# A hybrid decoder layer on one core: first-stage stores on GpSimd's queue, layer norm of two thirds on VectorE in column slices

## The chip, the cores and the metric

One Trainium2 chip, one core of it. The time is the device time of one execution in microseconds (us); a kernel's time is the median over its runs. Engines are named as the profile names them: PE (TensorE, matmuls; PEld its weight loads), DVE (VectorE), ACT (ScalarE), POOL (GpSimd) and SP (SyncE, which issues most DMAs).

## What is computed

One inference step of a decoder layer for 1024 prompt rows and 64 sample rows (together T = 1088), model width 2048, all in fp32:

```
h = x @ w_in + b_in              # q, k, v of two attention mixers, gates z and g: 78 tiles of 128 columns
q, k = rope(q), rope(k)          # first quarter of each head
o_a = sliding-window attention (window 128, sinks); o_b = 3 dilated groups, combined by their log-denominators
y_a, y_b = o_a * silu(z_a), o_b * silu(z_b)
m = sigmoid(g_a) * (y_a @ w_br_a) + sigmoid(g_b) * (y_b @ w_br_b)
y = LayerNorm(alpha * x + m @ w_out) * ln_g + ln_b
```

Besides y, the k and v of the step and the caches shifted by 8 rows are outputs, so part of the work is copying the old caches from HBM to HBM.

## The kernel before, in words

Every fp32 matrix product is made of three fp32r products: each operand is split into a rounded part (hi) and a rest (lo). For the weights this is done on the fly: SP loads 512 KB of weights into `wraw` (L78), ACT casts a piece of 128x512 to `whi` (L89), DVE subtracts it to get `wlo` (L90), and PE works on that piece (a "unit") with twelve matmuls. `Weights.ahead` (L100) asks for pieces some units ahead of PE, as far as 4 (first stage) or 6 (last stage) buffers of `whi` and `wlo` and 2 or 3 of `wraw` allow.

The order is written out by hand: one engine's instructions run in the order in which the program emits them. `tick` (L136) counts steps of PE's work, and `after(n, f)` (L132) emits f's instructions n ticks later. One tick is one unit against one chunk of columns in the first two stages (twelve matmuls), one whole unit in the last.

1. **First stage** (0 to about 861 us): `in_proj` (L164) over 34 tiles of q, k and v, twelve ticks each, columns in three chunks (384, 384, 320). `evac_qkv` (L266) takes each chunk out of PSUM, applies rope, and splits q and k into `hi` and `lo`, which have one buffer each, so the next tile writes where this one was. `store` (L310, L347) and `store_kv` (L328) then write to HBM: five DMAs for each of 20 q tiles, eleven for each of 7 k tiles, seven for each of 7 v tiles. `tick_q` (L371) adds a copy of a piece of old cache (up to 510 KB) every fourth tick, 96 in all. All these 322 DMAs are issued by SP, in one order with the weight loads.
2. **Second stage** (to about 2114 us): `in_proj` over the 44 gate tiles, with attention, decoding and merging emitted beside it, a step per tick. GpSimd does the attention's reductions over partitions (L446, L460) and issues the decode's loads. The attention's first loads are L396 (k), L409 (q) and L403 (v).
3. **Last stage**: three thirds of the columns, `CHUNKS`. For each third a *branch part* of 16 feature tiles, three units each (L1015 to L1017, 48 ticks; after each tile DVE does L1023, L1024, L1025 and, behind ACT's cast L1027, L1031), then an *output part* with 64 units (L1058 to L1060). After it `evac_out` (L1066) forms h and its statistics. The norm of the last third is done at the end of the program; the norm of the first two thirds is put into the next third's branch part, by `after` at the loop's end (L1115 to L1119): `norm_start` (L972) on DVE, then `norm_beside` (L984) on GpSimd, four operations of 128x2048 for each of three row tiles, and one store of 1 MB per tile.

Of the kernel before, what the change touches and what calls it, by code (L numbers as in the profile page):

```python
# [19 lines left out]
P = 128  # L20
DM = 2048
KT = DM // P
NT = 1024
NB = 8
NQ = 8
# [3 lines left out]
HD = 64  # L29
# [76 lines left out]
def layer_kernel(ctx: ExitStack, tc: tile.TileContext, A, O, S):  # L106
    nc = tc.nc
# [24 lines left out]
    def after(n, f):  # L132

        later.append((now[0] + n, f))
# [75 lines left out]
    with tc.tile_pool(name="qp", bufs=2, side="right") as qp:  # L210
# [55 lines left out]
        def evac_qkv(ft, c, a, b, pt):  # L266
            kind, idx, dil = FT[ft]
            n, e = b - a, min(b, NT)
            m = e - a
            bcol = bias[:, ft:ft + 1]  # L270
            if kind == "v":
                if c == 0:
                    held["f"] = qp.tile([P, T], F32, tag="kv", name="kvf", bufs=3)
                f = held["f"]
                nc.scalar.activation(cm(f, dil, a, e), nat(pt, dil, m), AF.Identity, bias=bcol)
                if e < b:
                    nc.scalar.activation(f[:, NT:], pt[:, m:n], AF.Identity, bias=bcol)
                    after(2, lambda: store_kv(1, idx, dil, f))
                    for h in range(2):
                        after(2 + h, lambda h=h: split_v(idx, f, h))  # L280
                return
            raw = qp.tile([P, 384], F32, tag="raw", name="raw")
            sw = qp.tile([P, 384], F32, tag="sw", name="sw")
            nc.scalar.activation(raw[:, :n], pt[:, :n], AF.Identity, bias=bcol)
            nc.vector.stream_shuffle(sw[:, :n], raw[:, :n], SWAP)
            nc.vector.tensor_mul(raw[:, :n], raw[:, :n], cost[:, a:b])
            nc.vector.tensor_mul(sw[:, :n], sw[:, :n], sint[:, a:b])
            if c == 0:
                held["hi"] = qp.tile([P, NT], F32R, tag="hi", name="qhi", bufs=1)
                held["lo"] = qp.tile([P, NT], F32R, tag="lo", name="qlo", bufs=1)  # L290
                if kind == "k":
                    held["f"] = qp.tile([P, T], F32, tag="kv", name="kvf", bufs=3)
            hi, lo, f = held["hi"], held["lo"], held.get("f")
            if kind == "q":
                nc.vector.tensor_add(raw[:, :n], raw[:, :n], sw[:, :n])
                src = nat(raw, dil, m)
            else:
                src = cm(f, dil, a, e)
                nc.vector.tensor_add(src, nat(raw, dil, m), nat(sw, dil, m))
                if e < b:  # L300
                    nc.vector.tensor_add(f[:, NT:], raw[:, m:n], sw[:, m:n])

            def split():
                nc.scalar.copy(cm(hi, dil, a, e), src)
                nc.vector.tensor_tensor(out=cm(lo, dil, a, e), in0=src, in1=cm(hi, dil, a, e).bitcast(F32),
                                        op=ALU.subtract)
                if e < b:
                    after(3, store)

            def store():  # L310
                if kind == "q":
                    nc.sync.dma_start(out=S["sq"][idx], in_=raw[:, m:n])
                    for t, x in enumerate((hi, lo)):
                        for h in range(2):
                            nc.sync.dma_start(out=S["qs"][idx, h, HD * t:HD * (t + 1)],
                                              in_=x[HD * h:HD * (h + 1)].bitcast(F32))
                else:
                    for t, x in enumerate((hi, lo)):
                        for j in range(4):
                            r = HD * (j // 2)  # L320
                            nc.sync.dma_start(out=S["ks"][2 * idx + j // 2, t, HD * (j % 2):HD * (j % 2 + 1)],  # L321
                                              in_=x[r:r + HD].bitcast(F32))
                    store_kv(0, idx, dil, f)
                    nc.sync.dma_start(out=S["sk"][idx], in_=f[:, NT:])

            after(1, split)

        def store_kv(kv, idx, dil, f):  # L328
            g, i = (0, 0) if idx == 0 else (1 + (idx - 1) // 2, (idx - 1) % 2)
            w = min(NT, 128 if g == 0 else WINS[g - 1])  # L330
            j = NT // dil
            nc.sync.dma_start(
                out=O[f"kv{g}"][kv, i].rearrange("p (c j) -> p c j", c=dil),
                in_=f[:, :NT].rearrange("p (c j) -> p c j", c=dil)[:, :, j - w // dil:])
            nc.sync.dma_start(out=O[f"kvs{g}"][kv, i], in_=f[:, NT:])

        def split_v(idx, f, half):
            pt = psa()
# [3 lines left out]
            v = pt.rearrange("p (j h d) -> p j h d", j=4, h=2)  # L342
# [3 lines left out]

            def store():  # L347
                for h in range(2):
                    nc.sync.dma_start(
                        out=S["vs"][2 * idx + h, :, 4 * half:4 * half + 4],  # L350
                        in_=vs[:, :, h].rearrange("p j s d -> p j (s d)").bitcast(F32))

# [4 lines left out]
            nc.tensor.transpose(pt[:NS, :P], f[:, NT:], ident)  # L357
            sv = qp.tile([NS, P], F32, tag="sv", name="sv")
            nc.scalar.copy(sv, pt[:NS, :P])
            nc.sync.dma_start(out=S["sv"][idx], in_=sv)  # L360

        copies = []
        for g in range(4):
# [7 lines left out]
        def tick_q():  # L371
            tick()
            if copies and now[0] > 30 and now[0] % 4 == 0:
                g, b, r, e = copies.pop(0)
                nc.sync.dma_start(out=O[f"c{g}"][b, r:e], in_=A[f"c{g}"][b, NQ + r:NQ + e])

        in_proj([ORDER[:2]] + [[ft] for ft in ORDER[2:34]], 0, evac_qkv, tick_q)
        while later or copies:
# [602 lines left out]
        nc.gpsimd.tensor_mul(h, h, lng[:h.shape[0], a:b])  # L981
        nc.gpsimd.tensor_add(h, h, lnb[:h.shape[0], a:b])

    def norm_beside(h, v):  # L984
        nc.gpsimd.tensor_sub(h, h, v[:, 0:1].to_broadcast([P, DM]))  # L985
        nc.gpsimd.tensor_mul(h, h, v[:, 2:3].to_broadcast([P, DM]))
        nc.gpsimd.tensor_mul(h, h, lng)
        nc.gpsimd.tensor_add(h, h, lnb)

    def norm_vector(h, v, a, b):  # L990
        h = h[:, a:b]
        nc.vector.scalar_tensor_tensor(out=h, in0=h, scalar=v[:, 0:1], in1=lng[:h.shape[0], a:b],
                                       op0=ALU.subtract, op1=ALU.mult)
        nc.vector.scalar_tensor_tensor(out=h, in0=h, scalar=v[:, 2:3], in1=lnb[:h.shape[0], a:b],
                                       op0=ALU.mult, op1=ALU.add)

    gi = 78 * 4
    for part, (a, b) in enumerate(CHUNKS):
# [113 lines left out]
        if not last:  # L1112
            after(2, lambda: nc.scalar.activation(m4[:, :, 2], m4[:, :, 1], AF.Sqrt, bias=epst))
            nxt = load_g(0, *CHUNKS[part + 1])
            for i, (t, c) in enumerate(tiles):  # L1115
                h, v = hs[i], mv[:, 4 * i:4 * i + 4]
                after(3, lambda v=v: norm_start(v))
                after(4 + i, lambda h=h, v=v: norm_beside(h, v))
                after(5 + i, lambda t=t, h=h: nc.gpsimd.dma_start(out=O["y"][t:t + P], in_=h))  # L1119
    while later:  # L1120
        tick()

# [127 lines left out]
```

## Time and profile before

| | |
|---|---|
| median of 3 runs | 2870.86 us (2870.16 to 2871.94) |
| the profiled execution | 2865.24 us, its span 2863.5 us |
| mean granted TensorE clock | 0.983 |
| busy share of the span | PE 96%, PEld 92%, DVE 53%, ACT 32%, POOL 27% |
| moved by DMA | 467.60 MB, 163 GB/s over the span |

The profile shows one execution. Its own time is 5.6 us under the median of the runs; spans and waits below are of this execution. The span is the time from its first to its last instruction. PE's busy time counts matmuls in flight, at whatever clock was granted, so a stretch can be long by idle time or by a low clock; the view by stretches shows both.

### The profile page before, as it was taken

The page shows a single profiled execution, that of the slowest core. Times are in us where ns is not written, and L with a number is a line of the kernel's source. Part 1 is how long each engine was busy: PE and PEld are TensorE (multiplying, and loading weights), DVE is VectorE, ACT ScalarE, POOL GpSimd, SP SyncE. Part 2 cuts the span into 40 slices and gives each one's busy share as a digit, 9 for nine tenths or more (in the row PEclk, how much of TensorE's full clock was granted, in tenths as well). Part 3 has the DMA queues.
Part 4 walks back from the last instruction along what each step waited for, and adds up shares of the span by engine and source line. Part 5 has one row for each costly group of instructions (what it writes and reads, how often), then busy time and mean ns, then how long its engine had stood idle before and what let it go on. Part 6 is the DMA issues. An engine that isn't in the chain of part 4 may idle for free.

```text
span 2863.5 us, 42950 instructions
## 1 busy us (share of the span) xinstructions
PE 2760.6 (96%) x16423; PEld 2641.7 (92%) x16423; DVE 1530.0 (53%) x2600; ACT 925.8 (32%) x1857; POOL 770.9 (27%) x589
## 2 busy tenths in 40 slices
PE   8999999999989999999999999999999996997898
PEld 8999999989989999999999998889899886986886
DVE  5444433423426778777665422116556458557856
ACT  4222222222223544444443321223144323432442
POOL 0000000000005666677677613432100025004201
PEclk9999999999999999999999999999999997998899
DMA  6345564465463333455445445559866535643662
GB/s 217 101 126 164 165 187 150 156 190 167 142 198 110 116 111 114 136 153 150 142 144 149 123 119 189 182 168 284 276 202 233 188 120 168 241 131 105 205 220 96
DMA packets 224965, 467.60 MB, mean 163 GB/s; under 512 B 33896, under 2 KB 151208, under 8 KB 221240
## 3 DMA queue, kind: packets, MB, share of 16 engines
q1 hardware_dynamic: 206264, 405.09, 45.0%
q0 software_dynamic: 16400, 52.43, 6.1%
q10 hardware_dynamic: 2096, 7.34, 0.7%
q8 instruction: 129, 2.11, 0.3%
q14 instruction: 76, 0.62, 0.1%
HBM read 365.17 MB, written 144.21 MB: 178 GB/s over the span
## 4 chain that ended last, share of the span: by engine, by line
PE 84%; DVE 6%; DMA 5%; SPq 2%; issue 1%; ACT 1%; POOL 0%; ACTq 0%; DVEq 0%; POOLq 0%
PE psd L170 19%; PE psd L172 18%; PE psd L171 18%; PE psd L1060 3%; PE psd L1059 3%; PE psd L1058 3%; PE psa L425 2%; PE psd L1017 2%; PE psd L1016 2%; PE psd L1015 2%; DMA wraw<-w_in 2%; DVE wlo L90 2%; SPq L321 1%; PE psa L487 1%; PE psa L486 1%
## 5 line engine op out<-in xcount | busy, mean ns | idle before, releaser
L170 PE MATMUL psd<-xhi,whi 128*128 128x384 f32 (+1 forms) x3712 | 1226.2, 330 | 26.4 <-ACT whi L89 23.8
L172 PE MATMUL psd<-xhi,wlo 128*128 128x384 f32 (+1 forms) x3712 | 1219.5, 329 | 2.1 <-DVE wlo L90 1.7
L171 PE MATMUL psd<-xlo,whi 128*128 128x384 f32 (+1 forms) x3712 | 1217.8, 328 | 0.3 <-DVE xlo L226 0.3
L90 DVE TENSOR_TENSOR wlo<-wraw,whi 128x512 fp32r<-128x512 f32 x648 | 482.2, 766 | 653.6 <-ACT whi L89 641.7
L170 PEld LDWEIGHTS psd<-xhi,whi 128*128 128x128 f32 x3712 | 699.9, 189 | 48.9 <-ACT whi L89 26.3
L172 PEld LDWEIGHTS psd<-xhi,wlo 128*128 128x128 f32 x3712 | 699.3, 188 | 5.7 <-DVE wlo L90 5.7
L171 PEld LDWEIGHTS psd<-xlo,whi 128*128 128x128 f32 x3712 | 699.7, 189 | 0.8 <-DVE xlo L226 0.8
L89 ACT CAST whi<-wraw 128x512 fp32r<-128x512 f32 x648 | 385.7, 618 | 592.2 <-DMA wraw<-w_in 348.8
L446 POOL PARTITION_ALL_REDUCE md<-s x160 | 214.6, 1341 | 1038.9 <-DMA vst<-s_vs 865.0
L460 POOL PARTITION_ALL_REDUCE md<-s x160 | 310.0, 1938 | 67.4 <-ACT s L457 44.2
L477 DVE TENSOR_TENSOR pl<-s,ph 128x512 fp32r<-128x512 f32 (+1 forms) x160 | 127.9, 800 | 100.4 <-ACT ph L476 98.4
L1017 PE MATMUL psd<-y,wlo 128*128 128x384 f32 (+1 forms) x384 | 129.1, 336 | 29.7 <-DVE wlo L90 29.7
L985 POOL TENSOR_TENSOR h<-h,mv 128x2048 f32<-128x2048 f32 x6 | 21.6, 3608 | 484.1 <-ACT whi L89 276.3
L1015 PE MATMUL psd<-y,whi 128*128 128x384 f32 (+1 forms) x384 | 129.1, 336 | 21.6 <-ACT whi L89 21.6
L1060 PE MATMUL psd<-wlo,m 128*128 128x512 f32 x384 | 149.8, 390 | 0.0
L1059 PE MATMUL psd<-whi,m 128*128 128x512 f32 x384 | 149.7, 390 | 0.0
L1058 PE MATMUL psd<-whi,m 128*128 128x512 f32 x384 | 149.6, 390 | 0.0
L457 ACT ACTIVATE s<-s 128x256 f32<-128x256 f32 (+1 forms) x160 | 75.9, 475 | 195.9 <-DVE s L456 193.8
L951 ACT ACTIVATE z<-psd,bias 128x384 f32<-128x384 f32 x132 | 73.8, 562 | 195.1 <-PE psd L172 129.4
L1016 PE MATMUL psd<-y,whi 128*128 128x384 f32 (+1 forms) x384 | 128.3, 334 | 0.0
L491 DVE TENSOR_TENSOR num<-psa,pvl 64x256 f32<-64x256 f32 x160 | 66.1, 413 | 77.3 <-ACT pvl L490 76.6
L1017 PEld LDWEIGHTS psd<-y,wlo 128*128 128x128 f32 x384 | 74.4, 194 | 32.1 <-DVE wlo L90 32.1
(202 smaller groups left out, 3183.4 us busy)
## 6 DMA issues: line engine op xcount, KB each, us to landing
wraw<-w_in SPq DMA_DIRECT2D x152, 512.0 KB
wraw<-w_out SPq DMA_DIRECT2D x96, 512.0 KB
wraw<-w_br SPq DMA_DIRECT2D x72, 512.0 KB
o_c<-c SPq DMA_DIRECT2D x64, 510.0 KB
qst<-s_qs SPq DMA_DIRECT2D x80, 256.0 KB
s_zg<-z SPq DMA_DIRECT2D x64, 192.0 KB
kv<-ktb POOLq DMA_DIRECT2D x48, 256.0 KB, 3.4
kv<-vb POOLq DMA_DIRECT2D x48, 256.0 KB, 3.1
```

The costliest lines, as they stand in the source:

```text
L89: self.nc.scalar.copy(hi, raw)
L90: self.nc.vector.tensor_tensor(out=lo, in0=raw, in1=hi.bitcast(F32), op=ALU.subtract)
L170: nc.tensor.matmul(o, lhsT=h, rhs=xhi[k][:, a:b], start=(k == 0), stop=False)
L171: nc.tensor.matmul(o, lhsT=h, rhs=xlo[k][:, a:b], start=False, stop=False)
L172: nc.tensor.matmul(o, lhsT=l, rhs=xhi[k][:, a:b], start=False, stop=(k == KT - 1))
L446: nc.gpsimd.partition_all_reduce(u["md"][:, 0], top, P, RED.max)
L460: nc.gpsimd.partition_all_reduce(u["md"][:, 1], s[:, 1 if n == 1 else 2], P, RED.add)
L1015: nc.tensor.matmul(o, lhsT=h, rhs=yt[k][:, 0, :n], start=st, stop=False)
L1017: nc.tensor.matmul(o, lhsT=l, rhs=yt[k][:, 0, :n], start=False, stop=en)
L1058: nc.tensor.matmul(pt, lhsT=h, rhs=whi, start=st, stop=False)
L1059: nc.tensor.matmul(pt, lhsT=l, rhs=whi, start=False, stop=False)
L1060: nc.tensor.matmul(pt, lhsT=h, rhs=wlo, start=False, stop=en)
```

## The change

Two independent edits. In the first stage every store and every cache copy is issued by GpSimd in place of SP (same transfers, same place in the program). In the last stage the norm of the first two thirds is done by DVE with two `scalar_tensor_tensor` operations per slice of 512 columns (subtract the mean and multiply by ln_g; multiply by the inverse deviation and add ln_b), one operation per tick, with a store of 256 KB per slice from GpSimd; `norm_vector`, which the last third uses, is split into the two functions.

```
         def store():
             if kind == "q":
-                nc.sync.dma_start(out=S["sq"][idx], in_=raw[:, m:n])
+                nc.gpsimd.dma_start(out=S["sq"][idx], in_=raw[:, m:n])
...
-                            nc.sync.dma_start(out=S["qs"][idx, h, HD * t:HD * (t + 1)],
+                            nc.gpsimd.dma_start(out=S["qs"][idx, h, HD * t:HD * (t + 1)],
...
-                            nc.sync.dma_start(out=S["ks"][2 * idx + j // 2, t, HD * (j % 2):HD * (j % 2 + 1)],
+                            nc.gpsimd.dma_start(out=S["ks"][2 * idx + j // 2, t, HD * (j % 2):HD * (j % 2 + 1)],
...
         def tick_q():
...
-                nc.sync.dma_start(out=O[f"c{g}"][b, r:e], in_=A[f"c{g}"][b, NQ + r:NQ + e])
+                nc.gpsimd.dma_start(out=O[f"c{g}"][b, r:e], in_=A[f"c{g}"][b, NQ + r:NQ + e])
...
-    def norm_beside(h, v):
-        nc.gpsimd.tensor_sub(h, h, v[:, 0:1].to_broadcast([P, DM]))
-        nc.gpsimd.tensor_mul(h, h, v[:, 2:3].to_broadcast([P, DM]))
-        nc.gpsimd.tensor_mul(h, h, lng)
-        nc.gpsimd.tensor_add(h, h, lnb)
-
-    def norm_vector(h, v, a, b):
+    def norm_scale(h, v, a, b):
         h = h[:, a:b]
         nc.vector.scalar_tensor_tensor(out=h, in0=h, scalar=v[:, 0:1], in1=lng[:h.shape[0], a:b],
                                        op0=ALU.subtract, op1=ALU.mult)
+
+    def norm_shift(h, v, a, b):
+        h = h[:, a:b]
         nc.vector.scalar_tensor_tensor(out=h, in0=h, scalar=v[:, 2:3], in1=lnb[:h.shape[0], a:b],
                                        op0=ALU.mult, op1=ALU.add)
...
                 after(3, lambda v=v: norm_start(v))
-                after(4 + i, lambda h=h, v=v: norm_beside(h, v))
-                after(5 + i, lambda t=t, h=h: nc.gpsimd.dma_start(out=O["y"][t:t + P], in_=h))
+                for u in range(0, DM, 512):
+                    n = 4 + 14 * i + 3 * (u // 512)
+                    after(n, lambda h=h, v=v, u=u: norm_scale(h, v, u, u + 512))
+                    after(n + 1, lambda h=h, v=v, u=u: norm_shift(h, v, u, u + 512))
+                    after(n + 2, lambda t=t, h=h, u=u: nc.gpsimd.dma_start(
+                        out=O["y"][t:t + P, u:u + 512], in_=h[:, u:u + 512]))
```

The stores of `sk`, `kv`, `kvs`, `vs` and `sv` change in the same way as the ones shown.

How the order moves, first on SP's queue in the first stage, around two k tiles that follow each other (`s_ks`, `s_sk`, `o_kv` and `o_kvs` are k's stores, `o_c<-c` a cache copy, `wraw<-w_in` a weight load). Before:

```order
L78 DMA wraw<-w_in 128x1024
L375 DMA o_c<-c 16x8160 x2
L321 DMA s_ks<-qhi 64x1024 x4
L321 DMA s_ks<-qlo 64x1024 x4
L332 DMA o_kv<-kvf 128x128
L335 DMA o_kvs<-kvf 128x64
L324 DMA s_sk<-kvf 128x64
L78 DMA wraw<-w_in 128x1024
L375 DMA o_c<-c 16x8160
L78 DMA wraw<-w_in 128x1024
```

On GpSimd's queue with the change, the last rows of the first stage and the first of the attention (`L446 ISA md<-s` is the first reduction, the bare `L446 ISA` stands ahead of it once):

```order
L332 DMA o_kv<-kvf 128x1024
L335 DMA o_kvs<-kvf 128x64
L360 DMA s_sv<-sv 64x128
L349 DMA s_vs<-vs 128x4x128 x2
L375 DMA o_c<-c 16x8160
L349 DMA s_vs<-vs 128x4x128 x2
L375 DMA o_c<-c 16x8160
L446 ISA
L446 ISA md<-s 128x256 x2
```

The stores and copies have gone from SP's queue, where nothing but weight loads is left between the constants and L396; on GpSimd they keep their order among each other and stand ahead of the attention's first reduction. Before, the bare `L446 ISA` is the first thing that GpSimd runs after the program's start.

Second, DVE in the last third's branch part, two feature tiles (`wlo` the weight split, `ga`, `gb` and `m` the tile's evacuation). Before:

```order
L90 TENSOR_TENSOR wlo<-wraw,whi 128x512 x3
L1023 TENSOR_TENSOR ga<-psd,ga 128x320
L1024 TENSOR_TENSOR gb<-psa,gb 128x320
L1025 TENSOR_TENSOR ga<-ga,gb 128x320
L1031 TENSOR_TENSOR m<-ga,m 128x256
L1031 TENSOR_TENSOR m<-ga,m 128x64
```

With the change (line numbers are one higher; `h<-h,mv,lng` and `h<-h,mv,lnb` are the norm's two operations):

```order
L90 TENSOR_TENSOR wlo<-wraw,whi 128x512
L986 SCALAR_TENSOR_TENSOR h_24104<-h_24104,mv,lng 128x512
L90 TENSOR_TENSOR wlo<-wraw,whi 128x512
L991 SCALAR_TENSOR_TENSOR h_24104<-h_24104,mv,lnb 128x512
L90 TENSOR_TENSOR wlo<-wraw,whi 128x512
L1024 TENSOR_TENSOR ga<-psd,ga 128x320
L1025 TENSOR_TENSOR gb<-psa,gb 128x320
L1026 TENSOR_TENSOR ga<-ga,gb 128x320
L1032 TENSOR_TENSOR m<-ga,m 128x256
L1032 TENSOR_TENSOR m<-ga,m 128x64
```

Two more operations stand between the splits of a feature tile, in 12 of the 16 tiles of a branch part (24 operations), in the second and in the last third; GpSimd's operations are gone from both.

## Rows read from the trace of the kernel before

**Rows 1.** The page, busy time of each engine: PE.

```profile
PE 2760.6 (96%) x16423; PEld 2641.7 (92%) x16423; DVE 1530.0 (53%) x2600; ACT 925.8 (32%) x1857; POOL 770.9 (27%) x589
```

**Rows 2.** Stretches: length, busy us of each engine, clock, DMA share, GB/s.

```profile
0.00:861.00 861.00, 838.11 (x5019) 830.75 (x5019) 341.51 (x665) 206.79 (x368) 0.19 (x4) 0.99 0.52 163
...
2114.50:2214.30 99.80, 99.80 (x578) 99.80 (x577) 64.84 (x111) 47.62 (x98) 0.00 (x0) 1.00 0.68 223
2344.90:2478.10 133.20, 107.24 (x578) 104.41 (x577) 108.59 (x123) 48.59 (x97) 52.47 (x15) 0.88 0.49 161
2608.60:2731.80 123.20, 93.08 (x577) 90.65 (x577) 105.63 (x138) 46.07 (x97) 52.07 (x15) 0.85 0.50 163
```

**Rows 3.** Waits of PE in 2340 to 2680 us: total, times, longest.

```profile
PE psd L1017 <- DVE wlo L90: 29.7, 6, 7.0
PE psd L1015 <- ACT whi L89: 21.6, 4, 8.6
```

**Rows 4.** The split L90: ns min/median/max, clean branch part and beside GpSimd.

```profile
L90 DVE TENSOR_TENSOR wlo<-wraw,whi x39: 683/692/695, 2131.1 to 2206.2; 128x512 fp32r<-128x512 f32 x39
...
L90 DVE TENSOR_TENSOR wlo<-wraw,whi x9: 678/4083/5045, 2348.5 to 2401.2; 128x512 fp32r<-128x512 f32 x9
```

**Rows 5.** DVE in order of time: start, us; and GpSimd's groups, 2340 to 2670.

```profile
2369.12 14.02 DVE L90 TENSOR_TENSOR wlo<-wraw,whi 128x512 fp32r<-128x512 f32 x3
...
L987 POOL TENSOR_TENSOR h<-h,lng 128x2048 f32<-128x2048 f32 x6 | 28.3, 4714 | 0.5
```

**Rows 6.** Waits of PE in 370 to 900 us.

```profile
PE psd L170 <- ACT whi L89: 10.7, 7, 3.4
PE psa L425 <- DMA qst<-s_qs: 3.0, 1, 3.0
```

**Rows 7.** In order of time, at the last k tile of the first stage.

```profile
807.34 1.23 SPq L321 DMA_DIRECT2D s_ks<-qhi  x1
...
816.45 0.44 SPq L78 DMA_DIRECT2D wraw<-w_in  x1
...
822.14 0.52 PE L170 MATMUL psd<-xhi,whi 128*128 128x384 f32 x1 [3.40 <-ACT whi L89]
```

**Rows 8.** Stretches of 10 us (columns as in rows 2).

```profile
820.00:830.00 10.00, 7.86 (x40) 7.39 (x41) 2.75 (x5) 5.15 (x11) 0.00 (x0) 0.83 0.62 231
...
860.00:870.00 10.00, 7.01 (x28) 6.72 (x27) 1.12 (x2) 0.62 (x1) 1.09 (x1) 0.67 0.45 144
```

**Rows 9.** GpSimd's DMA issues, ns min/median/max; last, o_y's issue to landing, us.

```profile
L663 POOL DMA_DIRECT2D kv<-vb x56: 537/537/578, 1726.0 to 1903.9; - x56
...
L661 POOL DMA_DIRECT2D kv<-ktb x56: 710/722/752, 1700.8 to 1875.8; - x56
...
DMA to landing us min/median/max: 4.2/5.9/7.6
```

**Rows 10.** ACT's evacuation of two q tiles that follow each other.

```profile
106.48 0.58 ACT L284 ACTIVATE raw<-psd,bias 128x384 f32<-128x384 f32 x1 [3.48 <-PE psd L172]
...
130.28 0.58 ACT L284 ACTIVATE raw<-psd,bias 128x384 f32<-128x384 f32 x1 [3.50 <-PE psd L172]
```

**Rows 11.** DVE in a clean feature tile of the last third's branch part.

```profile
2705.64 0.49 DVE L1024 TENSOR_TENSOR gb<-psa,gb 128x320 f32<-128x320 f32 x1 [0.36 <-PE psa L1017]
...
2707.71 1.29 DVE L90 TENSOR_TENSOR wlo<-wraw,whi 128x512 fp32r<-128x512 f32 x2
...
2709.47 0.69 DVE L90 TENSOR_TENSOR wlo<-wraw,whi 128x512 fp32r<-128x512 f32 x1 [0.46 <-ACT whi L89]
...
2710.92 0.49 DVE L1024 TENSOR_TENSOR gb<-psa,gb 128x320 f32<-128x320 f32 x1 [0.36 <-PE psa L1017]
```

**Rows 12.** The same in a clean feature tile of the second third's.

```profile
2444.95 0.69 DVE L90 TENSOR_TENSOR wlo<-wraw,whi 128x512 fp32r<-128x512 f32 x1 [0.57 <-ACT whi L89]
...
2447.07 0.56 DVE L1024 TENSOR_TENSOR gb<-psa,gb 128x384 f32<-128x384 f32 x1 [0.96 <-PE psa L1017]
```

**Rows 13.** The operation's kind at the new width.

```profile
2343.74 0.69 DVE L1072 SCALAR_TENSOR_TENSOR h<-h,psd 128x512 f32<-128x512 f32 x1 [1.60 <-PE psd L1060]
```

More of the change, by code (lines that the diff above doesn't have):

```diff
@@ L320, in store @@
                             r = HD * (j // 2)
-                            nc.sync.dma_start(out=S["ks"][2 * idx + j // 2, t, HD * (j % 2):HD * (j % 2 + 1)],
+                            nc.gpsimd.dma_start(out=S["ks"][2 * idx + j // 2, t, HD * (j % 2):HD * (j % 2 + 1)],
                                               in_=x[r:r + HD].bitcast(F32))
                     store_kv(0, idx, dil, f)
-                    nc.sync.dma_start(out=S["sk"][idx], in_=f[:, NT:])
+                    nc.gpsimd.dma_start(out=S["sk"][idx], in_=f[:, NT:])
             after(1, split)
@@ L331, in store_kv @@
             j = NT // dil
-            nc.sync.dma_start(
+            nc.gpsimd.dma_start(
                 out=O[f"kv{g}"][kv, i].rearrange("p (c j) -> p c j", c=dil),
                 in_=f[:, :NT].rearrange("p (c j) -> p c j", c=dil)[:, :, j - w // dil:])
-            nc.sync.dma_start(out=O[f"kvs{g}"][kv, i], in_=f[:, NT:])
+            nc.gpsimd.dma_start(out=O[f"kvs{g}"][kv, i], in_=f[:, NT:])
         def split_v(idx, f, half):
@@ L348, in store @@
                 for h in range(2):
-                    nc.sync.dma_start(
+                    nc.gpsimd.dma_start(
                         out=S["vs"][2 * idx + h, :, 4 * half:4 * half + 4],
@@ L359, in split_v @@
             nc.scalar.copy(sv, pt[:NS, :P])
-            nc.sync.dma_start(out=S["sv"][idx], in_=sv)
+            nc.gpsimd.dma_start(out=S["sv"][idx], in_=sv)
         copies = []
@@ L993, in norm_vector @@
                                        op0=ALU.subtract, op1=ALU.mult)
+    def norm_shift(h, v, a, b):
+        h = h[:, a:b]
         nc.vector.scalar_tensor_tensor(out=h, in0=h, scalar=v[:, 2:3], in1=lnb[:h.shape[0], a:b],
                                        op0=ALU.mult, op1=ALU.add)
+    def norm_vector(h, v, a, b):
+        norm_scale(h, v, a, b)
+        norm_shift(h, v, a, b)
     gi = 78 * 4
```

## The prediction

> **What bounds the kernel now.** I read the page first. PE is in flight for 2760.6 us of the span [rows 1], so the program is bound by matmuls, and what an edit of stores and of a norm can give is PE's idle time, 102.9 us, and what PE loses at a low clock. The view by stretches says where that is. The first third's branch part is clean: 99.8 us long, PE busy for all of it, clock 1.00. The second third's part has the same matmuls and takes 133.2 us, with PE busy 107.24 us at a mean clock of 0.88; the last third's, with 320 columns in place of 384, takes 123.2 us, PE busy 93.08, clock 0.85 [rows 2]. The two long ones are the two in which GpSimd works, 52.47 and 52.07 us. The first stage, 861 us, has another 22.9 us of idle PE, part of it at the very start, before the first loads have landed.
>
> Next, the waits. Around the two long parts PE waits for the weights' splits, 29.7 us for DVE's half (`wlo`) and 21.6 for ACT's (`whi`) [rows 3]. The reader should see that this is not lack of work on DVE: a split takes 0.69 us in the clean part, and a median of 4.08 us in the second third's [rows 4]. In order of time three splits take 14.02 us beside GpSimd operations of 4.71 us [rows 5]: the two engines take turns, a whole instruction each. [...]
>
> In the first stage the waits of PE between 370 and 900 us are 10.7 us for `whi` and 3.0 us for the attention's first q load [rows 6]. The order of time shows why: from 807.34 to 816.45 SP issues the eleven stores of a k tile, and only then the weight load behind them; PE stands still until 822.14, for 3.40 us [rows 7]. After such a gap the clock is down: 0.83 over 820 to 830 (620 to 630 reads the same), 0.67 over 860 to 870, where the q load is late [rows 8].
>
> **The change, part by part.** *The norm leaves GpSimd.* What it removes is the length of the two branch parts above a clean one. Second third: 133.2 - 99.8 = 33.4 us. For the last third there is no clean part of 320 columns, but its end is clean: from one L1024 to the next 5.28 us [rows 11], times 16 tiles 84.5 us, and 123.2 - 84.5 = 38.7. Together 72.1 us, low clock included.
>
> What it adds is 24 operations of 128x512 on DVE in each of the two parts, 2 per feature tile in 12 of 16 tiles. One of this kind and width takes 0.69 us [rows 13], and back to back two operations of that width take 1.29 [rows 11], so a tile gets 1.29 us more. Whether that costs anything is read from DVE's idle time in a clean tile that does not depend on the order: in the second third's part it waits 0.57 us for `whi` and 0.96 us for PE [rows 12], 1.53 us, more than 1.29, so nothing is late: 0. In the last third's these are 0.46 and 0.36, together 0.82 us [rows 11]; 1.29 - 0.82 = 0.47 us per tile are too much, 5.6 us over 12 tiles. DVE enters the part with some units split ahead, at 5.28 / 3 = 1.8 us of PE each, and a part of that is left after the evacuation of h; I take 4 us. The bounds are 0 (the head start covers it) and 12 x 1.29 = 15.5 us for each part (no idle time is usable).
>
> The stores of y go from 6 to 24, each issued by GpSimd in about 0.6 us, and GpSimd has nothing else there: 0. They add one wait: the loads of the next h on SP (L1036) wait for the last slices' stores. The last is issued about four ticks before the branch part ends and lands some 5.9 us later [rows 9], so SP may stand for a few us with weight loads behind it; the weights loaded and split ahead, several units of 1.8 us or more, cover that. If they did not, it would be at most 5.9 us per part; I take 0. So the norm gives 72.1 - 4 = 68 us.
>
> *The first stage's stores leave SP.* That is 20 x 5 + 7 x 11 + 7 x 7 = 226 stores and 96 copies, 322 DMAs. SP keeps weight loads alone, which go out as soon as DVE frees a buffer. What can go: the 10.7 and 3.0 us of waits [rows 6], and at half rate 0.17 x 10 twice and 0.33 x 10 once, 6.7 us [rows 8]: 20.4 us. The q load is among it, since the rows in front of it on SP become weight loads that are issued well ahead of PE.
>
> On GpSimd an issue costs 0.54 to 0.72 us [rows 9], 322 of them 174 to 232 us of 861 in which it is idle today (0.19 us busy [rows 2]). A tile's burst must land before the next tile's split overwrites `hi` and `lo`: a tile takes 130.28 - 106.48 = 23.8 us [rows 10], twelve ticks of 1.98, and the stores are emitted seven ticks, 13.9 us, ahead of the next split. A k tile needs 8 x 0.72 = 5.8 us to issue what reads these buffers and some 5.9 us to land, 11.7 us: it fits with 2 us left, and a late split is covered by units split ahead. The last stores and the bare ISA row now stand ahead of the attention's first reduction; the trace does not show what that row costs, since it runs at the start today. DVE needs the first result only some ticks later, so I take 0, with 0 and about 6 us (three ticks) as bounds. [...] I take 20 us of the 20.4, with a lower bound of 0.
>
> **The sum.** 68 + 20 = 88 us. On the profiled execution's own time, 2865.24, that is 2777; the median of the runs is 5.6 us higher, and on it 2870.9 - 88 = **2783 us**.
>
> [...] Rows first: beside DVE's splits and evacuations in decoding, the 112 issues of kv loads took 537 and 722 ns in the median, with a maximum of 578 and 752 [rows 9]: none waited for DVE. [...]
>
> **The rivals.**
> - *GpSimd's queue becomes the first stage's pace (slower).* Place: the issues between two tiles; a late store keeps `hi` and `lo`, and ACT and DVE, then PE, wait. It decides from 861 / 322 = 2.67 us per issue. The farthest price in the rows is what a DVE split paid beside GpSimd, 4.08 us [rows 4]: 1314 us, 453 more than the stage, less 68, a time of 3256 us. Even an issue that waits out one DVE operation each time, 0.72 + 0.69 = 1.41 us, stays hidden. Against it stand rows 9. Chance 0.04.
> - *The first stage gives nothing.* The 8 us of stores are still moved through the same 16 DMA engines, and the weight load waits there rather than on SP, or the buffers `hi` and `lo` come free too late and the wait moves to ACT. For it: DMA share 0.62 around the gap [rows 8]. Against it: the load lost its time on SP's queue, before it was issued [rows 7]. Only the norm is left: 2870.9 - 68 = 2803 us. Chance 0.14.
> - *DVE becomes the bound of both branch parts.* DVE runs in order and the idle time is not where the new operations stand: 15.5 us more in each, the norm gives 72.1 - 31 = 41, with the first stage's 20 61 us: 2810 us. For it: the last third's part has too little idle time by its own rows. Against: `whi` would be ready earlier when DVE is behind. Chance 0.10.
> - *The change does nothing of weight* (what it frees is lost in waits that I don't see): 2871 us. The order shows that GpSimd's operations are gone from both parts, so 0.02.
>
> **How the numbers follow.** The forecast has 0.70, the rivals 0.04, 0.14, 0.10 and 0.02. The forecast's own span runs from all of it, 2870.9 - 72.1 - 20.4 = 2778, to some 2795; below, 5.6 us for the profile that was faster than the median and the small waits not counted take it to 2770. Above, the second and third rival take it to 2810. So 2770 to 2810. A measurement of this kernel can tell about 0.2%, 5.7 us, from no change. Faster by more than that: 0.70 + 0.14 + 0.10 = 0.94; within it 0.02; slower 0.04.
>
> **What would show it.** Right: the branch parts of the last two thirds near 100 and 89 us, splits of 0.69 us there, the clock near 1.00, and GpSimd with DMA issues alone; in the first stage no wait of PE for `whi` at the k tiles and none of L425 for its q load, weight loads landed before DVE asks; on GpSimd issues below 1 us. Wrong: PE waiting for `wlo` all through the second third's part (DVE is the bound), first-stage waits of ACT or DVE for `s_ks` or `s_qs` stores (buffers), or issues on GpSimd of 2 us and more, with late stores.

## The result and the profile after

The changed kernel takes **2775.36 us** (median of 4 runs, 2774.55 to 2777.61); the kernel before, run beside it, 2870.51 (4 runs, 2867.98 to 2871.94). The ratio is 0.9671, with a 95% interval of 0.9654 to 0.9687: 95 us faster. The forecast was 2783, its range 2770 to 2810. The profiled execution took 2775.58 us, its span is 2773.7 us and its mean clock 0.996. From the norm on, line numbers of the changed kernel are one higher in the branch and output parts (L1016 to L1018, L1059 to L1061), and the norm's two operations are L986 and L991.

The page of the changed kernel, busy time of each engine; it answers to [rows 1]:

```profile
PE 2738.2 (99%) x16423; PEld 2626.4 (95%) x16423; DVE 1478.6 (53%) x2648; ACT 928.3 (33%) x1857; POOL 855.2 (31%) x905
```

PE is now in flight for 2738.2 of 2773.7 us: of 102.9 us of idle PE 35.5 are left. VectorE's busy time fell from 1530.0 to 1478.6 us although 48 operations of some 0.75 us were added to it: in the branch parts it no longer spends time inside its instructions waiting for GpSimd (a split takes 0.69 us there, see below).

Stretches of the changed kernel (length, then busy us of PE, PEld, DVE, ACT and POOL, then clock, DMA share, GB/s): the later part of the first stage, then the branch parts of the second and the last third, then the last output part and the end. The second and third row answer to [rows 2]:

```profile
300.00:850.00 550.00, 549.22 (x3344) 548.61 (x3343) 212.61 (x415) 131.24 (x235) 131.64 (x234) 1.00 0.53 173
2323.60:2423.50 99.90, 99.90 (x578) 99.88 (x577) 82.52 (x147) 48.53 (x97) 6.51 (x12) 1.00 0.68 214
2554.00:2639.60 85.60, 85.44 (x578) 84.53 (x577) 75.50 (x156) 43.68 (x92) 6.48 (x12) 1.00 0.71 227
2639.60:2773.70 134.10, 117.87 (x513) 95.78 (x512) 81.08 (x120) 43.84 (x78) 9.48 (x6) 0.95 0.46 155
```

In both branch parts PE is busy for all but 0.2 us at most, at clock 1.00; before, they were 33.3 and 37.7 us longer. The only wait of PE that is left between 300 and 850 us (total, times, longest), where [rows 6] had 10.7 and 3.0 us:

```profile
PE psa L341 <- ACT kvf L275: 0.8, 1, 0.8
```

By the start of each part (the first L425, L1016, L1059) the two profiled executions compare so, in us (the starts are read to 0.01 us, so a length can differ by 0.1 from that of a window above):

| part | before | after | difference |
|---|---|---|---|
| first stage, to the first L425 | 864.0 | 840.0 | -24.0 |
| second stage | 1250.5 | 1253.2 | +2.7 |
| first third, branch and output | 230.4 | 230.4 | 0.0 |
| second third, branch | 133.2 | 99.8 | -33.3 |
| second third, output | 130.6 | 130.6 | 0.0 |
| last third, branch | 123.2 | 85.5 | -37.7 |
| last third, output and end | 131.6 | 134.1 | +2.5 |
| span | 2863.5 | 2773.7 | -89.8 |

VectorE's groups in the last third's branch part (count, then busy us, mean ns of one, then idle time before them); the split L90 answers to [rows 4], the two norm operations to [rows 13]:

```profile
L90 DVE TENSOR_TENSOR wlo<-wraw,whi 128x512 fp32r<-128x512 f32 x45 | 29.9, 687 | 1.6 <-ACT whi L89 1.5
L991 DVE SCALAR_TENSOR_TENSOR h<-h,mv,lnb 128x512 f32<-128x512 f32 x12 | 9.0, 746 | 0.0
L986 DVE SCALAR_TENSOR_TENSOR h<-h,mv,lng 128x512 f32<-128x512 f32 x12 | 9.0, 746 | 0.0
```

A split takes 0.69 us again, where [rows 4] had a median of 4.08 beside GpSimd. GpSimd's DMA issues of the first stage, same columns; they answer to [rows 9]:

```profile
L375 POOL DMA_DIRECT2D o_c<-c x96 | 47.5, 499 | 9.2 <-DMA s_ks<-qlo 4.9 <-issue 3.0 <-DMA s_ks<-qhi 1.0
L349 POOL DMA_DIRECT2D s_vs<-vs x28 | 21.7, 777 | 8.5 <-DVE vs L345 8.4
L315 POOL DMA_DIRECT2D s_qs<-qhi x40 | 21.4, 539 | 0.9
...
L321 POOL DMA_DIRECT2D s_ks<-qlo x28 | 14.6, 528 | 0.0
```

They take 0.50 to 0.78 us in the mean and 0.86 us at most, together 178 us of the stage's 840, beside a VectorE that is busy for 212.61 of 550 us. What VectorE runs between the first of these issues (55.4 us) and the attention's start is splits, other operations of two tensors, and shuffles (L285, 0.57 us in the mean).

### The profile page after: what moved, and what is told of

Same layout as the page of the kernel before. It is cut to its first block, busy times and chain, and to the rows that moved or that the text cites. A ratio compares the mean times of both kernels' runs of the same rounds, so it can differ in the third digit from the quotient of the medians.

```text
span 2773.7 us, 43073 instructions
## 1 busy us (share of the span) xinstructions
PE 2738.2 (99%) x16423; PEld 2626.4 (95%) x16423; DVE 1478.6 (53%) x2648; ACT 928.3 (33%) x1857; POOL 855.2 (31%) x905
## 4 chain that ended last, share of the span: by engine, by line
PE 91%; DMA 5%; DVE 2%; issue 1%; ACT 0%; POOL 0%; SPq 0%; ACTq 0%; DVEq 0%; POOLq 0%
PE psd L170 21%; PE psd L172 20%; PE psd L171 20%; PE psd L1059 3%; PE psd L1060 3%; PE psd L1061 3%; PE psa L425 2%; PE psd L1016 2%; PE psd L1017 2%; PE psd L1018 2%; DMA z<-s_z 1%; PE psa L487 1%; PE psa L486 1%; PE psa L1016 1%; PE psa L1017 1%; PE psa L1018 1%
## 5 line engine op out<-in xcount | busy, mean ns | idle before, releaser
L170 PE MATMUL psd<-xhi,whi 128*128 128x384 f32 (+1 forms) x3712 | 1223.0, 329 | 16.5 <-ACT whi L89 14.5
L170 PEld LDWEIGHTS psd<-xhi,whi 128*128 128x128 f32 x3712 | 698.3, 188 | 37.1 <-issue 18.7
L90 DVE TENSOR_TENSOR wlo<-wraw,whi 128x512 fp32r<-128x512 f32 x648 | 449.0, 712 | 483.1 <-ACT whi L89 470.9
L446 POOL PARTITION_ALL_REDUCE md<-s x160 | 214.4, 1340 | 177.5 <-DVE s L435 66.0
L1123 POOL DMA_DIRECT2D o_y<-h x24 | 13.0, 542 | 573.1 <-DVE h L991 562.5
L1059 PE MATMUL psd<-whi,m 128*128 128x512 f32 x384 | 149.8, 390 | 1.5 <-ACT whi L89 1.5
L1061 PE MATMUL psd<-wlo,m 128*128 128x512 f32 x384 | 149.7, 390 | 0.0
L312 POOL DMA_DIRECT2D s_sq<-raw x20 | 11.5, 576 | 372.3 <-DVE raw L295 372.3
L1018 PE MATMUL psd<-y,wlo 128*128 128x384 f32 (+1 forms) x384 | 125.8, 328 | 0.2
L1016 PE MATMUL psd<-y,whi 128*128 128x384 f32 (+1 forms) x384 | 125.4, 327 | 0.0
L1017 PE MATMUL psd<-y,whi 128*128 128x384 f32 (+1 forms) x384 | 125.4, 327 | 0.0
L284 ACT ACTIVATE raw<-psd,bias 128x384 f32<-128x384 f32 (+1 forms) x79 | 44.1, 559 | 199.4 <-PE psd L172 199.4
```

Of the source, the lines that this page charges most:

```text
L90: self.nc.vector.tensor_tensor(out=lo, in0=raw, in1=hi.bitcast(F32), op=ALU.subtract)
L170: nc.tensor.matmul(o, lhsT=h, rhs=xhi[k][:, a:b], start=(k == 0), stop=False)
L446: nc.gpsimd.partition_all_reduce(u["md"][:, 0], top, P, RED.max)
L1016: nc.tensor.matmul(o, lhsT=h, rhs=yt[k][:, 0, :n], start=st, stop=False)
L1018: nc.tensor.matmul(o, lhsT=l, rhs=yt[k][:, 0, :n], start=False, stop=en)
L1059: nc.tensor.matmul(pt, lhsT=h, rhs=whi, start=st, stop=False)
```

## The experiments

Twelve kernels ran, four on one chip each time, beside the kernel before on that chip (medians 2866.10, 2867.77 and 2867.17 us). Ratios are to that. These medians and the 2870.51 us beside the changed kernel differ by up to 4.4 us for one and the same kernel, so small differences are read from the parts of one profiled execution of each, of which this is the table (us; "end" is from the last third's first L1059 to the end of the span):

| kernel | median | ratio, 95% interval | first L425 | second stage | branch, second third | branch, last third | end |
|---|---|---|---|---|---|---|---|
| queue only | 2845.61 | 0.9925 (0.9902 to 0.9948) | 840.2 | 1250.3 | 133.2 | 123.3 | 131.5 |
| norm only | 2799.35 | 0.9771 (0.9743 to 0.9798) | 861.9 | 1253.9 | 99.8 | 85.3 | 134.9 |
| copies only on GpSimd | 2908.46 | 1.0147 (1.0124 to 1.0170) | 969.8 | 1255.7 | 99.8 | 85.9 | 135.7 |
| k stores only on GpSimd | 2784.27 | 0.9713 (0.9690 to 0.9735) | 843.6 | 1255.4 | 99.8 | 85.3 | 137.8 |
| norm sliced on GpSimd | 2804.88 | 0.9777 (0.9760 to 0.9795) | 840.4 | 1256.9 | 107.2 | 103.7 | 133.6 |
| no norm | 2771.05 | 0.9663 (0.9647 to 0.9679) | 839.5 | 1255.9 | 99.8 | 84.5 | 132.1 |
| norm twice | 2798.87 | 0.9763 (0.9748 to 0.9777) | 841.1 | 1252.5 | 106.3 | 102.1 | 137.8 |
| ScalarE's queue | 2793.46 | 0.9742 (0.9727 to 0.9756) | 856.6 | 1255.9 | 99.8 | 85.3 | 134.7 |
| loads of num on GpSimd | 2790.83 | 0.9726 (0.9702 to 0.9749) | 839.4 | 1260.0 | 99.8 | 85.3 | 136.2 |
| stores only on GpSimd | 2781.41 | 0.9698 (0.9674 to 0.9721) | 839.8 | 1251.6 | 99.8 | 85.3 | 138.0 |
| old norm, tiles spread | 2843.91 | 0.9915 (0.9891 to 0.9939) | 840.0 | 1254.2 | 133.2 | 123.6 | 131.5 |
| norm uncut on VectorE | 2796.11 | 0.9748 (0.9725 to 0.9772) | 840.3 | 1252.9 | 108.8 | 96.2 | 131.5 |

The end holds the time in which the last store lands, 3.9 to 8.8 us after VectorE's last operation, which differs from execution to execution; up to PE's last matmul the last output part takes 117.4 us in the kernel before and 119.4 in the changed one.

The theory: in the branch parts GpSimd's tensor operations and VectorE's take turns (the 0.69 and 4.08 us of a split in [rows 4]), and taking them off GpSimd gives some 71 us; in the first stage bursts of stores stand ahead of weight loads in SP's order, and that gives 24; the two do not touch each other. Diffs are against the changed kernel.

**1. Each half alone.** First the queue without the norm (the old `norm_beside` and its calls put back):

```diff
-                for u in range(0, DM, 512):
...
+                after(4 + i, lambda h=h, v=v: norm_beside(h, v))
+                after(5 + i, lambda t=t, h=h: nc.gpsimd.dma_start(out=O["y"][t:t + P], in_=h))
```

> The first stage's 322 stores and copies on GpSimd's queue, the layer norm as before (four GpSimd operations of 128x2048 in a row for each of six tiles). Theory (the two halves of the change do not touch each other, and the first stage alone gives 24 us): about 2847, 2842 to 2852; first L425 near 840, branch parts of the second and last third 133 and 123 as before. Rival (the first stage's gain is only an earlier start that attention or merging gives back, or part of it came with the norm's half): 2860 or more. Rival (the norm's half was less than its rows show, the queue more): under 2835.

Then the norm without the queue (all nine `gpsimd.dma_start` of the first stage back to SP):

```diff
-                    nc.gpsimd.dma_start(out=S["sq"][idx], in_=raw[:, m:n])
+                    nc.sync.dma_start(out=S["sq"][idx], in_=raw[:, m:n])
...
```

> The norm on VectorE in column slices, the 322 stores and copies on SP as before. Theory: the branch parts fall to about 100 and 86 us and the rest stays, so about 2870.5 - 71 = 2799, 2796 to 2804; first L425 near 864. Rival (halves not additive: with the first stage as before, the gain of the norm is smaller or larger by over 6 us): under 2793 or over 2806.

Measured 2845.61 and 2799.35, both as the theory has it. On their chip the halves save 20.5 and 66.8 us, together 87.2; the whole change saves 95.2 on its own. The product of the two ratios is 0.9698, near 0.9671, and by the intervals of the three the two can't be told apart. In the table each half leaves the other's parts untouched. Norm only keeps the first stage's waits of PE; these, in 370 to 900 us, answer to [rows 6]:

```profile
PE psd L170 <- ACT whi L89: 10.2, 7, 3.5
PE psa L425 <- DMA qst<-s_qs: 2.1, 1, 2.1
```

Its first stage ends at 861.9 us and not at 864.0, in the same program up to there: profiled executions of it differ by some 2 us, so the queue's 24.0 is 22 to 24.

**2. Which of the 322 DMAs matter.** Copies only: the 226 stores back to SP, line 375 left on GpSimd. k stores only: all but line 321 back to SP. Stores only: line 375 alone back to SP:

```diff
-                nc.gpsimd.dma_start(out=O[f"c{g}"][b, r:e], in_=A[f"c{g}"][b, NQ + r:NQ + e])
+                nc.sync.dma_start(out=O[f"c{g}"][b, r:e], in_=A[f"c{g}"][b, NQ + r:NQ + e])
```

> The change's norm; of the 322, only the 96 cache copies (DRAM to DRAM) go through GpSimd, the 226 stores of the results stay on SP. Theory (the stalls come from the bursts of small k stores that stand ahead of the weight loads in SP's order): the k tiles' stalls stay, first L425 at 856 to 864, time 2792 to 2800. Rival (the cache copies are what the weight loads and the loads of q stand behind): first L425 near 840 to 844, time 2775 to 2780.

> The change's norm; of the 322, only the 56 stores of k by heads (the line S[ks]) go through GpSimd, the other stores and the copies stay on SP. Theory (the k bursts are the larger part): the PE waits on weights in 370 to 850 go, first L425 between 841 and 850, time 2776 to 2786; the wait for the first q, 3.0 in the kernel before, may stay. Rival (all 322 count alike by their sum on SP's queue): a sixth of the 24 us, first L425 near 860, time about 2795.

> The changed kernel with the 96 cache copies back on SP; the 226 stores stay on GpSimd. Theory (SP's order stalls on the bursts of stores, and copies come one at every fourth tick): within 5 us of the changed kernel, 2774 to 2780, first L425 at 840 to 843. Rival (the copies on SP delay weight loads as much as stores do): first L425 at 847 or later, 2782 or more.

k stores alone: the first L425 at 843.6, so 56 of 322 DMAs bring 18.3 of the 21.9 us between norm only and the whole change. The waits for weights are gone, and the wait for q stays, as expected; among PE's waits in 370 to 900 us:

```profile
PE psa L425 <- DMA qst<-s_qs: 2.8, 1, 2.8
```

Stores only: the first L425 at 839.8, where the whole change has it. Its median, 2781.41, is 1.4 us past the expected interval, but the intervals of its ratio and of the whole change's (0.9654 to 0.9687) overlap. In the profiled execution (2777.59 us, the fastest of the four) no part is longer except the end, where the last store's landing differs: from VectorE's last operation (2766.64) to the end of the span 8.8 us, in the changed kernel (2769.18) 4.5. So once the stores have left SP, moving the copies, too, brings nothing that can be measured.

Copies only missed both theories by over 100 us: 2908.46, the first L425 at 969.8. Its stretches of 25 us, same columns as above:

```profile
25.00:50.00 25.00, 3.03 (x9) 1.60 (x7) 3.78 (x4) 2.23 (x3) 6.81 (x14) 0.60 0.97 329
50.00:75.00 25.00, 11.60 (x45) 10.29 (x46) 3.88 (x3) 3.30 (x3) 6.81 (x14) 0.58 1.01 370
...
175.00:200.00 25.00, 25.00 (x154) 25.00 (x153) 10.91 (x24) 5.67 (x12) 0.00 (x0) 1.00 0.44 128
```

And GpSimd in order of time at the start (start, us):

```profile
1.27 4.22 POOL L375 DMA_DIRECT2D o_c<-c  x8 [0.83 <-POOLq L1219]
...
57.98 0.49 POOL L375 DMA_DIRECT2D o_c<-c  x1 [1.31 <-DMA o_c<-c]
```

With the stores gone from GpSimd nothing paces its queue: the copies, which the program emits one every fourth tick, are issued as fast as earlier ones finish, all 96 in the first 150 us. The DMA engines are full (share 0.95 to 1.01 up to 150 us), PE gets as little as 3.03 us of work in 25, and from 25 to 150 us its clock is 0.58 to 0.65. What is starved is above all the first load of x: in the chain that ended last loads `xraw<-xT` are 5% of the span of 2907.9 us, some 145 us. In the changed kernel the copies stand behind stores that wait for computed data, and go out from 68.8 to 834.8 us; SP's order does the same in the kernel before, from 72.3 to 855.4 us. So the stores' bursts are what the change had to move; the copies may go along because stores stand between them.

**3. Does the queue matter?** All nine lines from GpSimd to ScalarE:

```diff
-                            nc.gpsimd.dma_start(out=S["ks"][2 * idx + j // 2, t, HD * (j % 2):HD * (j % 2 + 1)],
+                            nc.scalar.dma_start(out=S["ks"][2 * idx + j // 2, t, HD * (j % 2):HD * (j % 2 + 1)],
...
```

> The changed kernel with the first stage's 322 stores and copies on ScalarE's queue and not GpSimd's. Theory (what counts is that SP's order holds no stores between the weight loads, not which queue takes them): first L425 near 840 to 846 and 2775 to 2785, a little over the changed kernel because ScalarE rounds the weights too and a store that waits for its data holds that up. Rival (it needs an engine with nothing else to do in that stage): ScalarE's casts of the weights wait behind stores, PE waits on whi, first L425 over 860, 2795 or more.

The first L425 at 856.6, 2793.46 us: the rival by its mechanism, though 3.4 and 1.5 us under the bounds that it had for L425 and the time. Only some 5 us of the 22 are gained. ScalarE in order of time at a k tile:

```profile
799.65 3.30 ACTq L321 DMA_DIRECT2D s_ks<-qhi  x4
803.00 4.03 ACTq L321 DMA_DIRECT2D s_ks<-qlo  x4
...
810.39 0.62 ACT L89 CAST whi<-wraw 128x512 fp32r<-128x512 f32 x1 [10.26 <-DMA s_ks<-qlo]
```

The burst that held up a weight load on SP holds up a weight cast here, which follows 10.26 us after the one before it; ahead of L170 PE waits 21.8 us for `whi` over the span, 23.8 in the kernel before and 14.5 in the changed one. So the queue matters: the stores go to an engine on which nothing that PE needs soon stands behind them.

**4. Engine or burst: what made the norm dear.** The norm sliced as in the change, but on GpSimd; the uncut norm on GpSimd with the tiles 14 ticks apart; the uncut norm on VectorE, one tick apart:

```diff
-                    after(n, lambda h=h, v=v, u=u: norm_scale(h, v, u, u + 512))
-                    after(n + 1, lambda h=h, v=v, u=u: norm_shift(h, v, u, u + 512))
+                    after(n, lambda h=h, v=v, u=u: pool_scale(h, v, u, u + 512))
+                    after(n + 1, lambda h=h, v=v, u=u: pool_shift(h, v, u, u + 512))
...
+                after(4 + 14 * i, lambda h=h, v=v: norm_beside(h, v))
...
+                after(4 + i, lambda h=h, v=v: norm_vector(h, v, 0, DM))
```

> The changed kernel with its norm in the same column slices at the same places, but on GpSimd (subtract, multiply, then multiply, add, 128x512 each). Theory (any GpSimd operation of two tensors holds up the VectorE operations that read two tensors, however it is cut): a slice's four operations still hold VectorE for about 4 x 1.2 us, the total is that of the uncut norm, and most of the 71 us stays lost unless the gaps between slices let the weights catch up: 2800 to 2846. Rival (the burst is what costs: four operations of 4.7 us in a row outlast the weights held ahead, slices of 1.2 us do not): 2776 to 2785, branch parts 100 and 86 to 88.

> The changed kernel with the old norm, four GpSimd operations of 128x2048 in a row for a tile, but the three tiles 14 steps apart and not one step apart. Theory (each 19 us row of operations outlasts the weights held ahead, so each tile costs nearly what it did): 2835 to 2847. Rival (what the slices bring over the uncut norm comes from the pauses between tiles, in which VectorE catches up): near the sliced norm on GpSimd, 2800 to 2815.

> The changed kernel with the norm on VectorE but uncut: two operations of 128x2048 a tile (about 2.7 us each by 4 x 0.69), the three tiles one step apart as in the kernel before. Theory (a burst of 16 us on VectorE is longer than the weights held ahead, and the idle time of 0.8 to 1.5 us a tile makes it up only later): branch parts 103 to 110 and 90 to 98 us, 2783 to 2800. Rival (VectorE's total work counts and not its order): 2775 to 2780.

All three medians lie in the intervals of the theory, and together they say more than it did. Branch parts of the second and last third: uncut on GpSimd 133.2 and 123.3, cut 107.2 and 103.7, uncut on VectorE 108.8 and 96.2, cut 99.8 and 85.5. Cutting alone, with GpSimd kept, brings 45.6 us; VectorE alone, uncut, 51.5; both 71.1. For the sliced norm the theory's interval was wide (2800 to 2846) and its mechanism wrong: it said that the total counts however it is cut, and that "most of the 71 us stays lost", but only 25.6 stay. The rival was wrong as well, which had branch parts of 100 and 86 to 88. Spreading the uncut tiles brings nothing (133.2 and 123.6; around those parts PE's waits are 31.5 and 20.1 us, [rows 3] has 29.7 and 21.6):

```profile
PE psd L1024 <- DVE wlo L90: 31.5, 6, 7.1
PE psd L1022 <- ACT whi L89: 20.1, 4, 8.6
```

Why the cut helps is in the length of a turn. Sliced on GpSimd, last third, VectorE's splits and GpSimd's four operations:

```profile
L90 DVE TENSOR_TENSOR wlo<-wraw,whi 128x512 fp32r<-128x512 f32 x46 | 48.2, 1091 | 4.3 <-ACT whi L89 4.2
```

```profile
L1001 POOL TENSOR_TENSOR h<-h,lng 128x512 f32<-128x512 f32 x12 | 18.9, 1572 | 0.9
L1002 POOL TENSOR_TENSOR h<-h,lnb 128x512 f32<-128x512 f32 x12 | 17.3, 1445 | 0.9
L997 POOL TENSOR_TENSOR h<-h,mv 128x512 f32<-128x512 f32 x12 | 15.7, 1312 | 6.0 <-DVE mv L973 5.2
L996 POOL TENSOR_TENSOR h<-h,mv 128x512 f32<-128x512 f32 x12 | 12.6, 1052 | 154.3 <-DVE mv L1088 154.1
```

GpSimd is busy for longer than uncut (64.5 us for 52.07), yet a split takes 1.09 us in the mean, 2.04 at most, and not 4: what a split can wait out is one GpSimd operation of 1.05 to 1.57 us in the mean, where it was one of 4.7. The splits' 48.2 us, against 29.9 in the changed kernel, are 18.3 more; the part is 18.2 longer. The slices also stand two operations to a tick, where the uncut norm has four in a row. Whether uncut operations with pauses between them would do as well was not tried, so the length of one operation and the number in a row are not told apart.

Uncut on VectorE, in order of time in the last third:

```profile
2571.66 0.69 DVE L90 TENSOR_TENSOR wlo<-wraw,whi 128x512 fp32r<-128x512 f32 x1
2572.27 2.34 DVE L986 SCALAR_TENSOR_TENSOR h<-h,mv,lng 128x2048 f32<-128x2048 f32 x1
2574.65 2.35 DVE L991 SCALAR_TENSOR_TENSOR h<-h,mv,lnb 128x2048 f32<-128x2048 f32 x1
2576.91 0.68 DVE L90 TENSOR_TENSOR wlo<-wraw,whi 128x512 fp32r<-128x512 f32 x1
```

One split per 5.25 us, three times in a row, where PE uses one per 1.8 us. Less work than in slices (2.34 + 2.35 us a tile for 4 x 1.49), but in a row it is longer than what is split ahead (PE waits 10.5 us for `whi` and 4.1 for `wlo` in the branch parts), and costs 9.0 and 10.7 us more than the slices do.

**5. What the norm on VectorE still costs.** "No norm" leaves both norm operations of the first two thirds out, so its y is not normalized there; "norm twice" adds a neutral one behind each:

```diff
-                    after(n, lambda h=h, v=v, u=u: norm_scale(h, v, u, u + 512))
-                    after(n + 1, lambda h=h, v=v, u=u: norm_shift(h, v, u, u + 512))
...
+                    after(n, lambda h=h, u=u: again(h, u, u + 512))
+                    after(n + 1, lambda h=h, u=u: again(h, u, u + 512))
```

> The changed kernel without the norm of the first two thirds: their y is stored as it stands before it (the last third's norm is left in). Theory (the slices on VectorE cost the second third nothing and the last third about 1 us): 0 to 3 us under the changed kernel, 2772 to 2776. Rival (VectorE sets the pace in the last third and holds the weights up later, in the output part): 5 us or more under it.

> The changed kernel with each norm operation on VectorE followed by one more of the same shape (it takes the larger of h times 1 and h, so it changes nothing): 48 more of about 0.7 us in the two branch parts. Theory (VectorE has 0.36 + 0.46 us idle of a tile's 5.28 in the last third and 0.57 + 0.96 in the second; 1.3 us more a tile is past both): the last third's branch part grows by 12 x 1.3 = 16 us less a head start of 5, the second third's by 12 x (1.3 - 1.5 + 1.3) = 13 less as much, so 2788 to 2803. Rival (VectorE's idle time is larger than its rows show, since the conversions can run ahead of need): under 2782.

Without the norm 2771.05, 4.3 us below the changed kernel and a little past the expected 3, but the ratios' intervals overlap (0.9647 to 0.9679 and 0.9654 to 0.9687). By parts: 0.0 us in the second third's branch, 1.1 in the last's (84.5 is the clean length worked out from [rows 11]), 2.0 in the last output part and the end, 3.1 together. Twice the norm: 2798.87, within the expected interval, the branch parts longer by 6.5 and 16.5 us. PE's waits in them, 11.8 of these 23.0 us, show that the room is used up:

```profile
PE psd L1020 <- ACT whi L89: 10.2, 15, 1.1
PE psd L1022 <- DVE wlo L90: 1.6, 10, 0.2
```

**6. A try at more.** The merge's loads of num go to GpSimd, too:

```diff
-                nc.sync.dma_start(out=num[:, :n], in_=S["num"][i + 4 * g, :, :n])
+                nc.gpsimd.dma_start(out=num[:, :n], in_=S["num"][i + 4 * g, :, :n])
```

> A try at a faster version: the changed kernel with the merge's loads of num (line 838), too, on GpSimd's queue. There SP waits 78 us for z and 70 us for VectorE before it issues what stands behind, and PE is idle for 10 us in that stage. If these 10 us come from SP's order as in the first stage: 2766 to 2772. Rival (the merge is bound by the transfers themselves, the DMA share there being 0.8 to 1.0, or GpSimd's own operations of the merge hold the loads up): 2774 to 2785.

2790.83, slower than the changed kernel; the second stage is 6.8 us longer by the profile, 3.1 above the longest of the other kernels (1256.9). The profiled execution, 2783.74 us, is the fastest of the four; the rest of the 15 us in the medians is not in it, nor explained. Waits of SP in 1880 to 2100 us, in this kernel and then in the changed one:

```profile
SPq L953 <- ACT z L951: 150.0, 24, 21.5
```

```profile
SPq L953 <- ACT z L951: 105.3, 23, 21.5
SPq L838 <- DVE z L864: 33.0, 5, 14.1
SPq L838 <- DVE w L855: 20.5, 5, 8.3
SPq L838 <- DMA num<-s_num: 17.3, 5, 8.6
```

The waits in front of the loads of num (L838) are gone from SP, and it waits longer for z instead; PE's waits in that stretch went from 9.9 to 13.4 us. Which of the two parts of the rival holds (the transfers, or GpSimd's own operations) was not told apart. No version here beats the changed kernel beyond what can be measured.

## Why the prediction was right

The mechanisms were those forecast, and the sum was 88 us where the profiled executions show 89.7 (2865.24 to 2775.58). Of the 7.6 us between 2783 and 2775.36, 5.6 are the median of before over its profiled execution, which the forecast carried over and the changed kernel doesn't have. By parts the norm gave 68.5 us (71.0 in the branch parts, less 2.5 behind them) for 68, and the first stage 24.0 for 20; that the sum is nearer than its terms owes something to luck, since the second stage took 2.7 us the other way.

- **The norm's removal, 72.1.** Shown: the parts fell by 33.3 and 37.7, and experiment 5 gives the clean last third as 84.5 us, the number worked out.
- **What it costs on VectorE, 0 and 4.** The 0 held (0.0). The 4 was taken for the last third's branch: measured 1.1 there and 2.0 in the output part behind it, where PE waits once for `whi` (1.5 us) and without the norm doesn't; that fewer weights are split ahead at that point is likely, but not shown. The size was about right, 3.1 for 4, the place mostly wrong. A norm operation takes 0.75 us, not 0.69: [rows 13] is an operation of the same kind with another second operand, in PSUM; what makes the difference is not shown, and the neutral one of experiment 5, on h alone, takes 0.69 us, too.
- **The stores of y, 0.** Held: in the second third's part the last slice's store is issued at 2410.72, and SP issues the three loads of the next h from 2420.91 on, in 1.42 us, without a wait for it.
- **The rival "DVE becomes the bound"** is false for the change and true at twice the norm, where the parts grow by 6.5 and 16.5 us. The room in the last third is nearly used.
- **The first stage, 20 of 20.4.** 22 to 24 were measured: the term was sized a little low. All named waits are gone. Up to the first L425 PE's idle time fell by 16.7 us (25.9 to 9.2), of which 13.7 were named and 1.3 lie in the first 40 us, before any store; its busy time fell by 7.3 (838.1 to 830.8), where 6.7 were reckoned for the low clock. The half rate of that term is in the trace of the kernel before: behind the gap of [rows 7] the granted clock is 0.50 from 823 to 825 us, where matmuls of 128x384 start 0.32 us apart, and 1.00 from 827 to 828, where they start 0.17 us apart. The step was too general in one point: it spoke of 322 DMAs that leave SP, and 56 of them, the k stores, bring five sixths of it (18.3 of 21.9 us), the other 170 stores nearly all of the rest, and the 96 copies nothing once the stores have gone.
- **Buffers and issues.** An issue costs 0.50 to 0.78 us on GpSimd, as [rows 9] let expect, and neither ACT nor DVE waits for `hi` or `lo` in a way that reaches PE. The slower rival had no ground.
- **The bare ISA row, 0 (bounds 0 and 6).** In the changed kernel, in order of time, the first reduction comes late behind the product that it reads:

```profile
840.46 0.42 DVE L442 TENSOR_TENSOR s<-psa,masks 128x256 f32<-128x256 f32 x1 [7.74 <-PE psa L425]
...
842.98 1.08 POOL L446 PARTITION_ALL_REDUCE md<-s  x1 [7.67 <-issue]
```

GpSimd stands 7.67 us for nothing that the profile shows, but 5.6 of these lie before its input is there, so the reduction starts 2.1 us after it; in norm only, where the queue is as before, 0.2 us after it (862.83 and 863.06). No wait of PE follows, so the 0 held. What the 7.67 us are, no run shows.

- **Not in the sum:** the second stage's 2.7 us. Its length is 1250.3 to 1256.9 us in all kernels here that leave it alone, so 2.7 us are within what separates these executions, and no effect of the change can be read from it.

## What to carry to other kernels

Look in the order of time at what stands in front of a load on its queue: a burst of small stores, though a sixth of the DMAs, can be most of the stall (18.3 of 21.9 us here). Moving it helps in full where nothing urgent stands behind it (22 to 24 us on GpSimd), and little where something does (some 5 us on ScalarE). Before a DMA changes queues, ask what paced it on the old one: copies without inputs ran as soon as nothing stood ahead of them (all 96 in the first 150 us). Work that takes turns with a just-in-time producer is cut and spread until no stretch of it is longer than what that producer has ahead, before its total is made smaller (on VectorE 4.69 us a tile in a row cost 9.0 and 10.7 us more than 5.96 us in slices).

## What the runs showed that was not expected

- 96 DRAM-to-DRAM copies on a queue of their own fill the DMA engines (share 0.95 to 1.01, 329 to 370 GB/s) for 150 us and delay the first stage by 108 us against norm only (969.8 and 861.9); the same copies between stores cost nothing (the first L425 at 840.0 us, and at 839.8 with the copies on SP).
- Beside VectorE's splits the same norm holds GpSimd for more time in slices than uncut (64.5 and 52.07 us in the last third) and yet costs PE less: 18.2 us for 37.7 over the changed kernel's part. The sum is not what counts here, but how long VectorE is held up at a time: a split takes 2.04 us at most beside the slices, and 5.02 beside the uncut norm (queue only).
- At the k tile shown, the store of k by heads takes ScalarE's queue 0.83 to 1.01 us an issue (3.30 and 4.03 us for four); the median is 0.61 and 1.11 us (hi and lo, 28 each) on SP in the kernel before, and 0.53 for both on GpSimd.
